# Row sums of masked spatial weights: a VectorE reduction with a round trip through DRAM in place of matmuls with ones

## The chip, the cores and the metric

The kernel runs on one core of one Trainium2 chip. The metric is the device time of one execution in microseconds (us). The engines are named as in the profile: PE (TensorE matmul), PEld (TensorE weight load), DVE (VectorE), ACT (ScalarE), POOL (GpSimd) and SP (SyncE, which issues most loads). Each engine works through its own instructions in program order and waits on semaphores of the others.

## The reference, cut to what matters

One decoder block for 512 positions of width 1024. Its combined input projection feeds two mixers. The change lies in mixer A, the spatial gating unit:

```
def chunked_gmlp(u, v, w_s, b_s, ln_g, ln_b):
    n = s // CHUNK                                   # 4 chunks of 128 positions
    v = layer_norm(v, ln_g, ln_b).reshape(bsz, n, CHUNK, A_GROUPS, A_GROUP_DIM)
    mask = jnp.tril(jnp.ones((CHUNK, CHUNK)))
    mixed = jnp.einsum('gts,bnsgc->bntgc', w_s * mask, v) + b_s.T[None, None, :, :, None]
    return u * mixed.reshape(bsz, s, A_WIDTH)
...
y_a = chunked_gmlp(gelu(a_u), gelu(a_v), gmlp_w_s, gmlp_b_s, gmlp_ln_g, gmlp_ln_b)
```

The layer norm's bias `ln_b` is the same for all positions. So its part of `mixed` is `ln_b[g, c]` times the sum over s of the masked `w_s[g, t, s]`. The kernel mixes only the normalized v, multiplies by `ln_g` afterwards, and adds a bias tile that holds `b_s[g, t] + ln_b[g, c] * rowsum[g, t]`. The change is about where the eight row-sum vectors of 128 come from and how they reach all 128 partitions.

## The kernel before, in words

All large products are done in three matmuls over split operands (`mm3`, lines 64 to 68): each fp32 operand is a rounded part `hi`, copied by ACT (line 134), and a remainder `lo`, subtracted by DVE or POOL (line 138). The weights come in chunks of 128x1024. `get` and `ensure` load up to three raw chunks ahead through SP and split a chunk two chunks before PE needs it, so what ACT, DVE, POOL and SP do is tied to the chunk that PE is at. The order on each engine is the order in which the program emits its instructions (`tc.manual_schedule()`); tables say at which chunk a small task is emitted.

The stretch of the change is this:

- The loop of lines 924 to 946 computes v (`a_v`) in two halves of 512 columns, four chunks each, with the token tile on the PSUM partitions: four banks 0 to 3 (tile name `pav`), one for each tile of 128 tokens. `VT` holds tasks for the eight chunks: loading the spatial weights (`load_ws`, `wmT`), masking them (`mask_ws`, on POOL), loading the bias rows (`load_bs`, `bsb`). After each half, ACT evacuates the four banks through a gelu (line 946).
- Then u (`a_u`) is computed in four groups of two chunks each by `opt_b` (calls in lines 1051 and 1052), with weights on the partitions. The groups use PSUM banks 0 and 1, then 2 and 3, and so on in turn (tile name `pb`). So the first group of u writes the banks from which the first two gelus of v read. For each chunk, `au_tasks` is emitted before the matmuls and `au_post` after them. Step 0 of `au_tasks` finishes the layer norm statistics (`ln_v`, then `rstd` on POOL), steps 1 and 2 apply it on ACT, step 3 finishes the bias tile (`bias_mix`). After the third chunk (step 2), `au_post` emits the two row-sum matmuls `rs_mm`. From step 3 on it emits the mixing matmuls (`mix_mm`), evacuated by DVE (`mix_ev`).
- In the background of the same chunks DVE runs a top-k (lines 766 and 770) and dot products for the modulation vectors (line 209). The operand of such a dot product, `mraw`, has one buffer in this stretch, so its next load is issued by SP when the last dot product is done.
- After u come seven products for the branch gates (`xround`, lines 1095 to 1138), which add and subtract intermediate sums in PSUM. One of them, `Z[1] + kept[3]` (line 1126), is done by DVE before the sixth product accumulates on it.

Of the kernel before, what the change touches and what calls it, by code (L numbers as in the profile page):

```python
# [9 lines left out]
F32 = mybir.dt.float32  # L10
# [16 lines left out]

@with_exitstack
def block_kernel(ctx: ExitStack, tc: tile.TileContext, x, x_t, c_row, positions, w_ada_t, w_first, w_in, w_blocks,
                 gmlp_w_s, gmlp_b_s, w_proj_a, w_proj_b,  # L30
                 w_out, w_ffn_in, w_ffn_out, final_norm_g, small, consts, out):
    nc = tc.nc
    T, V, A, P, SY = nc.tensor, nc.vector, nc.scalar, nc.gpsimd, nc.sync
# [262 lines left out]
    KZ = ([0, 1, 2, 3, 4, 5, 6, 7, 12, 13, 20], [8, 9, 10, 11, 16, 17, 18, 19, 14, 15, 21])  # L296
    NZ = 6

    wsum = {n: dram.tile([11 * 128, 512], F32, name=f"wsum{n}") for n in (1, 2, 3, 4)}
    gdr = {n: dram.tile([8, 128], F32, name=f"gdr{n}") for n in (2, 5)}  # L300
    W_Z = {}
# [306 lines left out]
    def rows_a(b):  # L608
        m = 32 * len(RB[b])
        rope_a(("r", b), rqt[b][:m], "q", m)  # L610

    def rows_b(b):
        rope_b(("r", b))
        for r, v in enumerate(RB[b]):
            P.dma_start(v, rqt[b][32 * r:32 * r + 32])
# [50 lines left out]
    def h_hi(key):  # L666
        HS[key] = h_home(key)
        A.activation(HS[key][0][0][0], h_part(key), AF.Copy)
# [230 lines left out]
    def mask_ws():  # L899
        P.affine_select(late["wmT"], late["wmT"], pattern=[[0, 8], [1, 128]], compare_op=OP.is_ge, fill=0.0, base=0,  # L900
                        channel_multiplier=-1)
        late["ones"] = mid.tile([128, 2, 128], F32, name="ones2", tag="ql", bufs=2)[:, 0]
        P.memset(late["ones"], 1.0)

    VT = {0: [load_ws, lambda: rows_a(1), lambda: rows_b(1)],
          1: [lambda: h_hi("S1"), lambda: h_hi("S4"), lambda: h_lo("S1"), lambda: h_lo("S4")],
          2: [lambda: rows_a(2), lambda: rows_b(2), lambda: h_hi("S3")],
          3: [lambda: h_lo("S3")],
          5: [mask_ws],
          7: [load_bs]}  # L910
    for _ in range(16):
        bg.append((1.4, topk_max))
# [11 lines left out]
    for h in range(2):  # L924
        pb = [bank(k, "pav") for k in range(4)]
        for i in W_AV[h]:
            for fn in VT.get(vs, []):
                fn()
            if vs % 2:
                x_move()  # L930
            if iu[1] < 24:
                idx_accs()
            else:
                run_bg(2.0)
            if vs in (5, 6):
                for tk in (2 * vs - 10, 2 * vs - 9):
                    ln_v(tk, 0)
            vs += 1
            hi, lo = get(i)
            for tk in range(4):  # L940
                opt_a_mm(pb[tk], tk, hi, lo, stream[i]["kts"], hT, 8)
            idx_mms(4 if vs > 2 else 3)
        if not vg:
            vg.extend(mid.tile([128, 2, D], F32, name=f"vg{i}", tag=f"P{i}", bufs=1) for i in range(2))
        for tk in range(4):
            A.activation(vg[tk // 2][:, tk % 2, h * 512:(h + 1) * 512], pb[tk], AF.Gelu_apprx_tanh)
# [33 lines left out]
            ylow.append(lambda: V.tensor_sub(yT[m][1], y, f(yT[m][0])))  # L980
        ylate.append((austep[0] - 1, hi))

    def rs_mm():
        late["rs"] = [bank(5 + k, "rs") for k in range(2)]
        for k, p in enumerate(late["rs"]):
            T.matmul(p, late["ones"], late["wmT"][:, 4 * k:4 * k + 4].rearrange("p a n -> p (a n)"), start=True, stop=True)

    def bias_mix():
        for m in range(8):
            b = late["bsb"][:, m]  # L990
            V.scalar_tensor_tensor(b, late["rs"][m // 4][:, 128 * (m % 4):128 * (m % 4) + 128], lnbc[:, m:m + 1], b,
                                   op0=OP.mult, op1=OP.add)

    ub = {}
    austep = [0, 0]
# [2 lines left out]
    def au_post():  # L998
        s = austep[1]
        austep[1] += 1  # L1000
        if s == 2:
            rs_mm()
        for m in AT.get(s, []):
            mix_mm(m)
        while ylate and ylate[0][0] < s:
            ylate.pop(0)[1]()

    def au_tasks():
        s = austep[0]
        austep[0] += 1  # L1010
        if s == 0:
            assert iu[1] == 24
            for tk in range(4):
                ln_v(tk, 1)
            rstd(rva, mva[:, :, 1], 4, 1.0)
            V.scalar_tensor_tensor(nmr, mva[:, :, 0], -1.0, rva, op0=OP.mult, op1=OP.mult)
        elif s < 3:
            ln_v2(2 * s - 2)
            ln_v2(2 * s - 1)
        elif s == 3:  # L1020
            bias_mix()
        while ylow:
            ylow.pop(0)()
        for m in AT.get(s - 1, []):
            mix_ev(m)
        while zlate:
            zlate.pop(0)()
        for _ in range(BG.get(s, 0)):
            run_bg(0.1)
        if s < 9:  # L1030
            x_move()
        elif s == 9:
            assert not xm
        elif s == 27:
            k_b()
        if s in (28, 29):
            at_split(s - 28)
# [961 lines left out]
    for tk in range(2):  # L1999
# [26 lines left out]
                finish(tk)  # L2026


_INS = ["x", "x_t", "c_row", "positions", "w_ada_t", "w_first", "w_in", "w_blocks", "gmlp_w_s", "gmlp_b_s",
        "w_proj_a", "w_proj_b", "w_out", "w_ffn_in", "w_ffn_out", "final_norm_g", "small", "consts"]  # L2030
_OUTS = [((1, 512, 1024), "float32")]

# [52 lines left out]
```

## Time and profile before

| what | value |
|---|---|
| time before, median of 3 runs | 797.27 us (793.59, 798.15, 797.27) |
| the profiled execution's own time | 795.42 us |
| span of the profiled execution | 793.5 us, mean granted TensorE clock 0.996 |
| busy: PE, PEld | 780.2 us (98%), 697.5 us (88%) |
| busy: DVE, ACT, POOL | 662.6 us (84%), 443.2 us (56%), 183.7 us (23%) |
| DMA | 155.05 MB, mean 195 GB/s |

The span is the time from the first to the last instruction that the profile holds; the execution's own time is 1.92 us longer. A share of busy time is a mean over the whole span. A row of the timeline has the start in us from the span's start, the duration, engine, line, operation, the written and read tiles, shapes, and how many instructions are merged; what stands in brackets at its end is the idle time of the engine before it and what ended it. Matmuls are pipelined: a 128x512 matmul is shown with 0.39 us, while the next one starts 0.23 us after it.

### The profile page before, as it was taken

The numbers are of one execution on the slowest core, as the hardware profiler recorded it, in microseconds if no ns is written. First come the engines' busy times: TensorE is split into PE (matmuls) and PEld (weight loads), VectorE is DVE, ScalarE is ACT, GpSimd is POOL, SyncE is SP. The second block draws the span as 40 slices with busy tenths as digits, with TensorE's granted clock in tenths as the row PEclk, the third lists the DMA queues.
The fourth block names the chain that finished last, engine by engine and source line by source line (L and its number), as shares of the span: only waits on it lengthen the run. The fifth ranks groups of instructions, "written<-read, shape, count | busy, mean of one in ns | idle before, by whom it ended". The sixth has DMA issues, their size and how long they took to land.

```text
span 793.5 us, 12600 instructions
## 1 busy us (share of the span) xinstructions
PE 780.2 (98%) x4747; PEld 697.5 (88%) x4747; DVE 662.6 (84%) x1114; ACT 443.2 (56%) x777; POOL 183.7 (23%) x220
## 2 busy tenths in 40 slices
PE   7999999999999999999999999999999999999996
PEld 6779988878998988988888899999999999878885
DVE  5988887678896899886788869899998888798877
ACT  6556445443453536666436576656655556576654
POOL 2064234574433401000020000313132122100001
PEclk9999999999999999999999999999999999999999
DMA  9949454889763733149682503989996977665764
GB/s 358 416 155 241 119 149 118 223 228 239 212 212 107 239 107 107 54 147 281 227 225 62 175 1 108 262 252 273 282 264 194 280 179 189 176 201 196 217 195 146
DMA packets 89886, 155.05 MB, mean 195 GB/s; under 512 B 7009, under 2 KB 54769, under 8 KB 89634
## 3 DMA queue, kind: packets, MB, share of 16 engines
q1 hardware_dynamic: 72976, 116.05, 44.3%
q0 software_dynamic: 15952, 37.17, 20.8%
q10 hardware_dynamic: 898, 1.04, 0.4%
q8 instruction: 37, 0.61, 0.3%
q14 instruction: 23, 0.19, 0.1%
HBM read 150.16 MB, written 33.56 MB: 232 GB/s over the span
## 4 chain that ended last, share of the span: by engine, by line
PE 78%; DVE 11%; ACT 4%; DMA 3%; issue 2%; POOL 0%; POOLq 0%; ACTq 0%; DVEq 0%; SPq 0%
PE R L66 7%; PE R L67 7%; PE R L68 7%; PE pb L66 7%; PE pb L67 7%; PE pb L68 7%; PE pfo L67 2%; PE pfo L68 2%; PE pfo L66 2%; DMA raw<-in_w_ffn_out_dram 2%; PE pav L66 2%; PE pav L67 2%; PE pav L68 2%; PE zx L1116 2%; PE zx L1119 2%
## 5 line engine op out<-in xcount | busy, mean ns | idle before, releaser
L134 ACT ACTIVATE hi<-raw 128x1024 fp32r<-128x1024 f32 (+1 forms) x111 | 114.4, 1031 | 80.5 <-PE pb L67 32.5
L138 DVE TENSOR_TENSOR lo<-raw,hi 128x1024 fp32r<-128x1024 f32 (+2 forms) x77 | 90.2, 1173 | 27.9 <-ACT hi L134 27.7
L138 POOL TENSOR_TENSOR lo<-raw,hi 128x1024 fp32r<-128x1024 f32 x27 | 69.0, 2558 | 101.1 <-ACT hi L134 70.4
L67 PE MATMUL pfo<-lo,za 128*128 128x512 f32 (+1 forms) x144 | 55.5, 385 | 0.2 <-DVE lo L138 0.2
L66 PE MATMUL pfo<-hi,za 128*128 128x512 f32 (+1 forms) x144 | 55.4, 385 | 0.0
L68 PE MATMUL pfo<-hi,za 128*128 128x512 f32 (+1 forms) x144 | 55.2, 384 | 0.0
L209 DVE CUSTOM_DVE_ANT_0 mraw<-mraw,scb,cols 128x1024 f32<-128x1024 f32 x24 | 37.6, 1566 | 11.1 <-DMA mraw<-in_w_ada_t_dram 11.1
L66 PE MATMUL R<-tb,sx 128*128 128x256 f32 x160 | 45.0, 281 | 0.3 <-ACT R L1820 0.3
L351 POOL COPY sm<-sm 128x1 f32<-128x1 f32 x36 | 26.4, 733 | 79.7 <-ACT sm L350 79.7
L67 PE MATMUL R<-tb,sx 128*128 128x256 f32 x160 | 44.6, 279 | 0.0
L68 PE MATMUL R<-tb,sx 128*128 128x256 f32 x160 | 44.6, 279 | 0.0
L66 PE MATMUL R<-tb,hi 128*128 128x256 f32 x160 | 44.6, 278 | 0.0
L67 PE MATMUL R<-tb,hi 128*128 128x256 f32 x160 | 44.6, 278 | 0.0
L68 PE MATMUL R<-tb,lo 128*128 128x256 f32 x160 | 44.6, 278 | 0.0
L66 PE MATMUL pb<-h,hi 128*128 128x512 f32 (+1 forms) x112 | 42.7, 381 | 0.0
L68 PE MATMUL pb<-h,lo 128*128 128x512 f32 (+1 forms) x112 | 41.9, 374 | 0.0
L67 PE MATMUL pb<-h,hi 128*128 128x512 f32 (+1 forms) x112 | 41.9, 374 | 0.0
L331 POOL DMA_DIRECT2D wsum<-in_w_ffn_out_dram x24 | 21.2, 885 | 76.0 <-DMA wsum<-wsum 42.0
L66 PEld LDWEIGHTS pfo<-hi,za 128*128 128x128 f32 x144 | 27.1, 188 | 6.1 <-ACT ps L1925 0.6
L67 PEld LDWEIGHTS pfo<-lo,za 128*128 128x128 f32 x144 | 27.1, 188 | 6.1 <-DVE lo L138 0.9
L68 PEld LDWEIGHTS pfo<-hi,za 128*128 128x128 f32 x144 | 27.1, 188 | 5.3
L66 PEld LDWEIGHTS R<-tb,sx 128*128 128x128 f32 x160 | 30.3, 189 | 0.7 <-ACT R L1820 0.5
(398 smaller groups left out, 2695.5 us busy)
## 6 DMA issues: line engine op xcount, KB each, us to landing
raw<-in_w_ffn_in_dram SPq DMA_DIRECT2D x44, 512.0 KB, 6.2
raw<-in_w_in_dram SPq DMA_DIRECT2D x30, 512.0 KB, 3.8
wsum<-in_w_ffn_out_dram POOLq DMA_DIRECT2D x30, 512.0 KB, 8.3
mraw<-in_w_ada_t_dram SPq DMA_DIRECT2D x24, 512.0 KB, 6.0
raw<-wsum SPq DMA_DIRECT2D x20, 512.0 KB, 3.7
s<-in_w_ada_t_dram SPq DMA_DIRECT2D x16, 512.0 KB, 8.8
raw<-in_w_ffn_out_dram SPq DMA_DIRECT2D x16, 512.0 KB, 4.6
xsum<-in_w_blocks_dram POOLq DMA_DIRECT2D x12, 512.0 KB, 6.4
```

What stands on the lines that cost most here:

```text
L66: T.matmul(o, wh, rh, start=start, stop=False, **kw)
L67: T.matmul(o, wh, rlo, start=False, stop=False, **kw)
L68: T.matmul(o, wlo, rh, start=False, stop=stop, **kw)
L134: A.activation(hi[:, :m], e["raw"][:, :m], AF.Copy)
L138: e["lo"].tensor_sub(lo[:, :m], e["raw"][:, :m], f(hi[:, :m]))
L209: V.tensor_tensor_reduce(out=raw[:, o], in0=raw[:, o], in1=c, scale=1.0, scalar=col if o.start else bias, op0=OP.mult, op1=OP.add, accum_o ...
L331: P.dma_start(wsum[n][o], src, accum_op=OP.add)
L351: P.tensor_copy(t, t)
L1116: T.matmul(Z[z][:, m], hi[:, j, cc], hh, start=start and j + m == 0, stop=False, skip_group_check=True)
L1119: T.matmul(Z[z][:, m], lo[:, j, cc], hh, start=False, stop=j == 3, skip_group_check=True)
```

## The change

A second copy of the spatial weights with the output position t on the partitions (`gmlp_w_n`, arranged by the host) is loaded by POOL (`load_wn`, emitted at chunk 2 of v) into the tile tag A1, masked by POOL (`mask_wn`, chunk 4), and summed over s by one DVE reduction (`row_sums`, chunk 6) into eight columns of `sm`. After the last matmuls of v, `rs_out` turns these columns into eight rows with a PE transpose, copies them with ACT to SBUF and writes them to DRAM from ACT's queue. At step 1 of u, `rs_in` reads them back on POOL's queue, broadcast to all partitions, as a 128x1024 tile in A1. `bias_mix` moves from step 3 to step 2 and becomes two DVE operations of 128x1024, in place of eight of 128x128 that read the row sums from PSUM. The two matmuls with ones, the memset of the ones and their PSUM banks go.

```diff
@@ mask_ws
-        late["ones"] = mid.tile([128, 2, 128], F32, name="ones2", tag="ql", bufs=2)[:, 0]
-        P.memset(late["ones"], 1.0)
+    def load_wn():
+        late["wn"] = mid.tile([128, 8, 128], F32, name="wn", tag="A1", bufs=1)
+        P.dma_start(late["wn"], gmlp_w_n)
+    def mask_wn():
+        P.affine_select(late["wn"], late["wn"], pattern=[[0, 8], [-1, 128]], compare_op=OP.is_ge, fill=0.0, base=0,
+                        channel_multiplier=1)
+    def row_sums():
+        V.tensor_reduce(sm[:, 0:8], late["wn"], op=OP.add, axis=AX.X)
+    def rs_out():
+        p = bank(7, "rsT")
+        T.transpose(p[:8, :128], sm[:, 0:8], ident)
+        gr = tiny.tile([128, 128], F32, name="gr", tag="gr", bufs=1)
+        A.activation(gr[:8], p[:8, :128], AF.Copy)
+        A.dma_start(rsd, gr[:8])
+    def rs_in():
+        late["rs"] = mid.tile([128, 8, 128], F32, name="rs", tag="A1", bufs=1)
+        P.dma_start(late["rs"], bass.AP(tensor=rsd.tensor, offset=rsd.offset, ap=[[0, 128], [128, 8], [1, 128]]))
@@ the loop over v, after the matmuls of a half and ahead of its gelus
+        if h:
+            rs_out()
@@
-    def rs_mm():
-        late["rs"] = [bank(5 + k, "rs") for k in range(2)]
-        for k, p in enumerate(late["rs"]):
-            T.matmul(p, late["ones"], late["wmT"][:, 4 * k:4 * k + 4].rearrange("p a n -> p (a n)"), start=True, stop=True)
     def bias_mix():
-        for m in range(8):
-            b = late["bsb"][:, m]
-            V.scalar_tensor_tensor(b, late["rs"][m // 4][:, 128 * (m % 4):128 * (m % 4) + 128], lnbc[:, m:m + 1], b,
-                                   op0=OP.mult, op1=OP.add)
+        V.tensor_mul(late["rs"], late["rs"], lnbc[:, :, None].to_broadcast([128, 8, 128]))
+        V.tensor_add(late["bsb"], late["bsb"], late["rs"])
@@ au_post
-        if s == 2:
-            rs_mm()
@@ au_tasks
-        elif s == 3:
+        if s == 1:
+            rs_in()
+        elif s == 2:
             bias_mix()
```

On ACT, where v ends and u begins, the rows before are these (`vg` is the gelu of v, `hi` the split of a weight chunk, `rl` an evacuation of the index scores):

```order
L750 ACTIVATE rl<-idx 128x256 x2
L134 ACTIVATE hi<-raw 128x1024
L946 ACTIVATE vg_1305<-pav 128x512 x2
L946 ACTIVATE vg_1306<-pav 128x512 x2
L134 ACTIVATE hi<-raw 128x1024
```

And this is the same place now:

```order
L751 ACTIVATE rl<-idx 128x256 x2
L134 ACTIVATE hi<-raw 128x1024
L919 ACTIVATE gr<-rsT 8x128
L920 DMA rsd<-gr 8x128
L971 ACTIVATE vg_1308<-pav 128x512 x2
L971 ACTIVATE vg_1309<-pav 128x512 x2
L134 ACTIVATE hi<-raw 128x1024
```

The copy of the turned row sums and the issue of their DMA stand ahead of all four gelus.

On PE the same place now reads as follows; the transpose stands between the last matmul of v and the first of u:

```order
L67 MATMUL pav<-lo,h_157 128x512
L68 MATMUL pav<-hi,h_159 128x512
L917 MATMUL rsT<-ident,sm 8x128
L66 MATMUL pb<-h_156,hi 128x512
L67 MATMUL pb<-h_158,hi 128x512
```

What ACT's copy waits for is thus an instruction that PE issues after all of v's matmuls.

On DVE, in the second and third chunk of u, the rows before are these (`mraw` is the dot product's operand, `m` and `sco` belong to the top-k):

```order
L209 ISA mraw,GG_88<-mraw,scb,cols 128x1024
L209 ISA GG_88 128x1
L991 SCALAR_TENSOR_TENSOR bsb<-rs,cols,bsb 128x128 x8
L766 MAX m_1696<-sco_640 128x8
L766 MAX m_1698<-sco_639 128x8
```

And now, one dot product and one round of the top-k earlier:

```order
L209 ISA mraw,GG_88<-mraw,scb,cols 128x1024
L209 ISA GG_88 128x1
L1009 TENSOR_TENSOR rs<-rs,cols 128x1024
L1010 TENSOR_TENSOR bsb<-bsb,rs 128x1024
L767 MAX m_1653<-sco_641 128x8
L767 MAX m_1655<-sco_640 128x8
```

The eight operations on PSUM rows have become two on SBUF tiles, behind the dot product of step 2.

## Rows read from the trace of the kernel before

**Rows 1.** The page: span and busy time of PE.
```profile
span 793.5 us, 12600 instructions
PE 780.2 (98%) x4747; PEld 697.5 (88%) x4747; DVE 662.6 (84%) x1114; ACT 443.2 (56%) x777; POOL 183.7 (23%) x220
```

**Rows 2.** Timeline of PE around the two row-sum matmuls.
```profile
172.29 0.39 PE L68 MATMUL pb<-h,lo 128*128 128x512 f32 x1
172.52 1.88 PE L986 MATMUL rs<-wmT,ones 128*128 128x512 f32 x4
...
174.46 0.40 PE L67 MATMUL pb<-h,hi 128*128 128x512 f32 x1
```

**Rows 3.** Timeline where v ends and u begins.
```profile
152.31 0.60 ACT L946 ACTIVATE vg<-pav 128x512 f32<-128x512 f32 x1
...
155.97 0.39 PE L68 MATMUL pav<-hi,h 128*128 128x512 f32 x1
...
156.42 0.39 PE L67 MATMUL pb<-h,hi 128*128 128x512 f32 x1
```

**Rows 4.** Timeline around another transpose with copy and DMA, of a modulation vector.
```profile
233.71 0.39 PE L68 MATMUL pb<-y,lo 128*128 128x512 f32 x1
233.93 0.27 PE L460 MATMUL mod<-ident,GG 128*8 128x128 f32 x1
234.24 0.27 ACT L462 ACTIVATE gr<-mod 8x128 f32<-8x128 f32 x1 [4.02 <-PE mod L460]
...
234.95 1.06 ACT L134 ACTIVATE hi<-raw 128x1024 fp32r<-128x1024 f32 x1 [0.44 <-ACT gr L462]
```

**Rows 5.** Timeline between the two halves of v.
```profile
130.98 2.07 ACT L946 ACTIVATE vg<-pav 128x512 f32<-128x512 f32 x4
...
131.63 0.19 PEld L66 LDWEIGHTS pav<-hi,h 128*128 128x128 f32 x1 [0.36 <-ACT vg L946]
...
131.97 0.39 PE L67 MATMUL pav<-lo,h 128*128 128x512 f32 x1
```

**Rows 6.** Timeline of the layer norm statistics and what follows them.
```profile
157.03 0.69 DVE L919 BATCH_NORM_STATS2 bst<-vg 128x6 f32<-128x512 f32 x1 [0.42 <-ACT vg L946]
...
157.75 0.21 DVE L921 BATCH_NORM_AGGREGATE mva<-bst 128x2 f32<-128x12 f32 x1
...
159.53 4.49 DVE L209 CUSTOM_DVE_ANT_0 mraw<-mraw,scb,cols 128x1024 f32<-128x1024 f32 x1
...
160.09 2.83 POOL L138 TENSOR_TENSOR lo<-raw,hi 128x1024 fp32r<-128x1024 f32 x1
```

**Rows 7.** DVE's groups by line and shape, 120 to 230 us: count, busy, mean ns, idle before.
```profile
L209 DVE CUSTOM_DVE_ANT_0 mraw<-mraw,scb,cols 128x1024 f32<-128x1024 f32 x9 | 18.4, 2048 | 8.8 <-DMA mraw<-in_w_ada_t_dram 8.8
...
L138 DVE TENSOR_TENSOR lo<-raw,hi 128x1024 fp32r<-128x1024 f32 x5 | 6.1, 1217 | 0.7 <-ACT hi L134 0.7
...
L673 DVE TENSOR_TENSOR hs<-xT,hs 128x1024 fp32r<-128x1024 f32 x1 | 3.4, 3430 | 0.0
...
L991 DVE SCALAR_TENSOR_TENSOR bsb<-rs,cols,bsb 128x128 f32<-128x128 f32 x8 | 2.1, 335 | 0.0
```

**Rows 8.** Timeline of DVE and PE around the sum that DVE adds in PSUM.
```profile
219.46 1.23 DVE L138 TENSOR_TENSOR lo<-raw,hi 128x1024 fp32r<-128x1024 f32 x1 [0.67 <-ACT hi L134]
...
221.21 0.69 DVE L1126 TENSOR_TENSOR zx<-zx,zk 128x512 f32<-128x512 f32 x1
...
222.82 0.28 PE L1116 MATMUL zx<-hs,hi 128*128 128x256 f32 x1
```

**Rows 9.** Timeline of POOL and DVE at the chunks of v.
```profile
135.75 2.75 POOL L138 TENSOR_TENSOR lo<-raw,hi 128x1024 fp32r<-128x1024 f32 x1 [6.02 <-ACT hi L134]
138.45 1.42 POOL L900 TENSOR_SCALAR_AFFINE_SELECT wmT<-wmT 128x1024 f32<-128x1024 f32 x1
...
151.11 1.07 DVE L753 SCALAR_TENSOR_TENSOR sco<-rl,wi,sco 128x256 f32<-128x256 f32 x2 [2.74 <-ACT rl L750]
```

**Rows 10.** DMA issues: size and median us from issue to landing.
```profile
bsb<-in_gmlp_b_s_dram POOLq DMA_DIRECT2D x1, 512.0 KB, 4.5
```

More of the change, by code (lines that the diff above doesn't have):

```diff
@@ L29, in block_kernel @@
 def block_kernel(ctx: ExitStack, tc: tile.TileContext, x, x_t, c_row, positions, w_ada_t, w_first, w_in, w_blocks,
-                 gmlp_w_s, gmlp_b_s, w_proj_a, w_proj_b,
+                 gmlp_w_s, gmlp_w_n, gmlp_b_s, w_proj_a, w_proj_b,
                  w_out, w_ffn_in, w_ffn_out, final_norm_g, small, consts, out):
@@ L297, in block_kernel @@
     NZ = 6
+    rsd = dram.tile([8, 128], F32, name="rsd")
     wsum = {n: dram.tile([11 * 128, 512], F32, name=f"wsum{n}") for n in (1, 2, 3, 4)}
@@ L901, in mask_ws @@
                         channel_multiplier=-1)
-        late["ones"] = mid.tile([128, 2, 128], F32, name="ones2", tag="ql", bufs=2)[:, 0]
-        P.memset(late["ones"], 1.0)
+    def load_wn():
[15 more added lines that the diff above has]
+        P.dma_start(late["rs"], bass.AP(tensor=rsd.tensor, offset=rsd.offset, ap=[[0, 128], [128, 8], [1, 128]]))
     VT = {0: [load_ws, lambda: rows_a(1), lambda: rows_b(1)],
           1: [lambda: h_hi("S1"), lambda: h_hi("S4"), lambda: h_lo("S1"), lambda: h_lo("S4")],
-          2: [lambda: rows_a(2), lambda: rows_b(2), lambda: h_hi("S3")],
+          2: [lambda: rows_a(2), lambda: rows_b(2), lambda: h_hi("S3"), load_wn],
           3: [lambda: h_lo("S3")],
+          4: [mask_wn],
           5: [mask_ws],
+          6: [row_sums],
           7: [load_bs]}
@@ L2026, in block_kernel @@
                 finish(tk)
-_INS = ["x", "x_t", "c_row", "positions", "w_ada_t", "w_first", "w_in", "w_blocks", "gmlp_w_s", "gmlp_b_s",
+_INS = ["x", "x_t", "c_row", "positions", "w_ada_t", "w_first", "w_in", "w_blocks", "gmlp_w_s", "gmlp_w_n", "gmlp_b_s",
         "w_proj_a", "w_proj_b", "w_out", "w_ffn_in", "w_ffn_out", "final_norm_g", "small", "consts"]
@@ L2072 @@
     given["gmlp_w_s"] = _np.asarray(inputs["gmlp_w_s"])[0].transpose(2, 0, 1)
+    given["gmlp_w_n"] = _np.asarray(inputs["gmlp_w_s"])[0].transpose(1, 0, 2)
     for name in _INS:
```

## The prediction

> **What bounds the kernel now.** I read the page first: PE is busy for 780.2 of 793.5 us [rows 1]. Then I read PE's timeline over the stretch from v to the gate branch (150 to 230 us): its matmuls follow each other without a gap, a 128x512 every 0.23 us. So there every 0.1 us that is taken from or put on PE's own sequence moves the end, and work on other engines counts only where PE comes to wait for it. Last I read the timelines of ACT, DVE and POOL in that stretch, to see how far ahead of PE they are.
>
> **What is removed from PE.** The last matmul before the row sums starts at 172.29, and the second one after them at 174.46 [rows 2]. Two steps between ordinary matmuls would be 0.45 us (155.97 to 156.42 is two such steps, rows 3). So the two row-sum matmuls (four instructions in the trace) cost 2.17 - 0.45 = 1.72 us, all of it on the path. This is what the change gives back.
>
> **What is added where v ends.** In the kernel before, the first gelu of v starts at 152.31, as soon as the first token tile is complete, while PE still works on the other three until 155.97; so u's first matmuls find banks 0 and 1 empty [rows 3]. Now a copy stands ahead of the gelus on ACT, and the copy waits for a transpose that PE issues after all of v's matmuls. ACT works in order, so all four gelus wait, and u's first matmul needs bank 0 from the first of them.
>
> The trace has both halves of that chain. The transpose of a modulation vector starts 0.22 us after the matmul before it, its copy 0.53 us after that same matmul, and ACT's next work, behind the DMA issue, 1.24 us after it [rows 4]. Between the halves of v PE already waits once for a gelu of this kind: the gelu starts at 130.98, PE's weight load is released at 131.63, and the second matmul starts at 131.97, 0.99 us after the gelu [rows 5]. Put together: last matmul of v 155.97, first gelu 155.97 + 1.24 = 157.21, second matmul of u 157.21 + 0.99 = 158.20, against 156.42 before [rows 3]. That is 1.78 us. The bank of the second output tile costs nothing more, since the four gelus of rows 5 take 2.07 us together, one every half microsecond, and PE spends three matmuls on the first bank.
>
> So the two terms on PE's own sequence cancel: -1.72 + 1.78 = +0.06 us. The bounds of the second term: 0.1 us if the gelus could pass the copy (the transpose's own slot on PE), and some 2.8 us if the DMA issue on ACT holds the gelus 1 us longer than in rows 4.
>
> **What the late gelus do to DVE.** The statistics of the four token tiles follow the gelus. Before, the last pair starts at 157.03 and 157.75, and DVE's dot product behind them at 159.53 [rows 6]. Now the first gelu ends at 157.81. Each tile takes 0.69 us for the statistics, 0.21 us for the aggregate and 0.1 us of starts, so 1.0 us; the last aggregate starts at about 161.6, 3.9 us later than before. The rsqrt on POOL, the dot product on DVE and the layer norm on ACT all move by these 3.9 us. Two things could then be late for PE.
>
> First the splits on POOL: the one that follows the statistics runs from 160.09 to 162.92 [rows 6], now from about 164.0 to 166.8. PE needs it in u's third chunk, which starts 23 steps of 0.227 us ahead of 172.29 [rows 2], at 167.1, and now 1.7 us later. That leaves 2 us, and the next splits have more: the broadcast read of the row sums, queued ahead of the next one, costs POOL an issue.
>
> Second the sums in PSUM. PE's sixth gate product starts at 222.82 and accumulates on a bank to which DVE adds at 221.21 for 0.69 us: done 0.92 us before. The split on which DVE waited just before was released by ACT after 0.67 us of idle time [rows 8]. So DVE may come to this place some 1.6 us late without any harm, and each further microsecond stops PE. Does DVE make up 3.9 us in 60? In this stretch it sits idle for 8.8 us, all of it waiting for the operand of the next dot product, in front of five of nine [rows 7]. But that operand has one buffer, and SP issues its load when the last dot product is done; a late one makes its successor's load late. So this idle time is no reserve, except where DVE's own work between two of them is longer than the load. I take 3.9 - 1.6 = 2.3 us, less 0.1 us for PE's own shift: 2.2 us of PE waiting at the sixth gate product. Bounds: 0 if the loads land faster, since the bias no longer stands in the interval where one was slowest, and 4.5 by the third rival.
>
> **The rest is covered.** The bias took DVE eight operations, 2.1 us; it becomes two of 128x1024 with two SBUF inputs, like the split of 1.22 us: 2.4 us [rows 7], one chunk earlier, while its reader is two chunks away. The reduction is one pass over 128x1024, which no row shows; its nearest row is that same 1.22 us, and bounds of 0.7 and 3.4 us (a statistics operation of half the width in rows 6, a delayed operation in rows 7) change little, as DVE idles for 2.74 us just after it [rows 9]. The second mask is 1.42 us on POOL and lies in 6.02 us of idle time [rows 9]; if that cover went, the split of 2.75 us behind it would move by 1.4 us. The broadcast read comes after a write of 4 KB, issued at about 157; the like broadcast of the bias rows landed in 4.5 us [rows 10]. It is issued at about 167, so lands at 172, and DVE asks for it behind its dot product at about 175: no wait, unless it takes 8 us. The chip reads 1 MB more, as two loads of 512 KB, some 9 us of one transfer's time against 74 us of traffic between 123 and 197; raw chunks are loaded two chunks ahead. I count nothing for it.
>
> **A rule against this change.** In this trace a two-input DVE operation of 128x1024 took 3.43 us instead of 1.22 us [rows 7]; it was one that ran beside a POOL split. The eight old operations, with one input in PSUM, took 335 ns each. The Trainium skill ("SBUF — State Buffer", section "Who interferes with whom") says that a DVE instruction with two SBUF inputs and a GpSimd instruction that reads SBUF shut each other out for a whole instruction. By that rule the new form of the bias is exposed where the old was not, and the trace agrees in those 3.43 us; what it would cost is the third rival below.
>
> **The sum.** 793.5 - 1.72 + 1.78 + 2.2 = 795.8 us of span, +2.3 us. The profiled execution itself took 795.42 us, below the median of 797.27 and above the lowest of 793.59. The four times of this kernel have a mean of 796.1 us, and I add the 2.3 us to that: 798.4 us.
>
> **The rivals.**
> 1. DVE makes up its delay, since the load of the operand takes less time than the work between two dot products once the bias has left that interval. Then only +0.06 us stays: 796.2 us. For it speaks that the longest interval held both the bias and the wait. Against it: four other intervals also end in a wait for the load.
> 2. The gelus do not hold PE for 1.78 us, because the copy or the DMA issue on ACT lets them start earlier; the row sums' 1.72 us come through, and DVE is hardly late: 794.4 us. Against it speak the order on ACT and rows 4 and 5.
> 3. Slower: DVE meets POOL's splits in the new place. The bias pair at about 175 runs beside a split of the fifth or sixth chunk, and one of its two operations takes 3.43 instead of 1.22 us, so DVE is late by 3.9 + 0.3 + 2.2 = 6.4 us. PE then waits 6.4 - 1.6 - 0.1 = 4.7 us at the sixth gate product: 800.9 us. It decides once DVE is over 5.5 us late there. For it: POOL has a split in every chunk of u. Against it: a split fills only about half of a chunk's 5.4 us, and DVE must come second.
>
> **How the numbers follow.** My forecast (PE waits 1 to 3.5 us at the gate product) has a chance of 0.50, by itself 797.0 to 799.8 us; the first rival 0.24, the second 0.09, the third 0.17. A measurement of this kernel can tell about 0.5%, 4 us, from no change. Forecast and first rival lie within it, and nearly all of the second; of the third four fifths are beyond it. With the spread of the runs shown (793.59 to 798.15) on top I give faster 0.04, same 0.78, slower 0.18. The range reaches from the second rival's time to a little above the third's: 794.4 to 802.5 us.
>
> **What would show it.** In the changed kernel's profile: no row-sum matmuls; all four gelus of v's second half back to back after the copy, and a wait of u's first weight load for a gelu, with u's second matmul 2.2 us after v's last (0.45 before); the reduction without a wait of PE behind it; the dot product behind the statistics at about 163.4; and a wait of the sixth gate product for DVE's sum, the only one of more than 0.5 us. I am wrong if that first gap is under 1 or over 3 us, if PE waits for POOL's third-chunk split, if DVE waits for the row sums to land, or if PE passes the sixth gate product without a wait.

## The result, and the profile after

The changed kernel takes 798.7 us (median of 20 runs, 794.22 to 805.67), the kernel before 794.19 us (20 runs beside it, 791.39 to 798.15). The ratio is 1.0060 with a 95% interval of 1.0040 to 1.0081, that is 4.8 us (3.2 to 6.4) slower. The forecast was +2.3 us. It came to nearly the measured time because it was put on a mean of 796.1 us, which lies 1.9 us above the median of the larger sample: two errors of about 2 us that cancel. So the nearness of the time is luck: the change itself is about twice the +2.3 us that was forecast, and +2.3 us lies below its interval. The middle of the ratio lies beyond the 0.5% that I had called no change, and its interval reaches from below that mark to above it.

The profiled execution took 798.21 us (795.42 before). Its page:

```profile
span 796.4 us, 12592 instructions
...
PE 778.9 (98%) x4744; PEld 696.6 (87%) x4744; DVE 665.2 (84%) x1109; ACT 442.9 (56%) x778; POOL 184.3 (23%) x222
```

PE is busy 1.3 us less and the span is 2.9 us longer [rows 1]. Since one execution differs from the next by some us over its 800, I compare a stretch in which all that the change does lies: from v's last matmul (L68 in both kernels) to the last block of eight matmuls of the gate product that the prediction calls the sixth. Before it is 71.56 us, from 155.97 [rows 3] to the second of these rows of PE's timeline (the first is used below):

```profile
219.05 1.11 PE L1119 MATMUL zx<-h,lo 128*128 128x256 f32 x8
...
227.53 1.11 PE L1119 MATMUL zx<-h,lo 128*128 128x256 f32 x8
```

After it is 232.70 - 155.75 = 76.95 us, so 5.39 us longer. What follows the stretch lies outside the change and took between 561.1 us (e2) and 567.1 us (e12) in the fourteen profiled executions, 566.0 before and 563.7 after; that is why the two spans differ by 2.9 us only. PE's timeline after:

```profile
155.75 0.39 PE L68 MATMUL pav<-hi,h 128*128 128x512 f32 x1
155.98 0.27 PE L917 MATMUL rsT<-ident,sm 128*8 128x128 f32 x1
157.59 0.50 PE L66 MATMUL pb<-h,hi 128*128 128x512 f32 x1 [1.34 <-ACT vg L971]
157.93 0.40 PE L67 MATMUL pb<-h,hi 128*128 128x512 f32 x1
...
218.81 1.10 PE L1137 MATMUL zx<-h,lo 128*128 128x256 f32 x8
221.47 0.39 PE L1134 MATMUL zx<-hs,hi 128*128 128x256 f32 x1 [1.55 <-ACT zx L1121]
...
226.44 0.35 PE L1134 MATMUL zx<-hs,hi 128*128 128x256 f32 x1 [1.79 <-DVE zx L1144]
...
228.97 1.91 PE L1137 MATMUL zx<-hs,lo 128*128 128x256 f32 x8
...
232.70 1.07 PE L1137 MATMUL zx<-h,lo 128*128 128x256 f32 x8
```

The reader is to see three things. The hold at u is there: from v's last matmul to u's second 2.18 us, against 0.45 [rows 3], so +1.73 us, which the missing row-sum matmuls [rows 2] give back. At 218.81 PE begins a block 0.24 us earlier than before (219.05), and it had ended v 0.22 us earlier (155.75 against 155.97), so hold and row sums have cancelled. Then come two waits, one for ACT at the product ahead of the sixth and one for DVE's sum at the sixth. And behind them a block of eight matmuls takes 1.91 us instead of 1.10: the granted clock falls, which the stretches of the profile show (the columns are window, its length, busy time of PE, PEld, DVE, ACT and POOL with instructions, granted clock, DMA share, GB/s; the third window is the second half of the one above it):

```profile
222.00:226.00 4.00, 2.65 (x22) 2.42 (x21) 4.00 (x4) 3.97 (x5) 1.40 (x1) 1.00 0.33 111
226.00:230.00 4.00, 3.56 (x21) 3.59 (x22) 4.00 (x11) 2.42 (x4) 3.65 (x2) 0.71 0.80 287
228.00:230.00 2.00, 2.00 (x11) 2.00 (x11) 2.00 (x7) 0.60 (x1) 2.00 (x2) 0.50 0.87 335
230.00:234.00 4.00, 4.00 (x31) 3.96 (x30) 4.00 (x7) 1.74 (x3) 1.47 (x1) 0.86 0.74 224
```

Before, the second of these windows has a clock of 1.00 and no idle time of PE:

```profile
226.00:230.00 4.00, 4.00 (x30) 3.74 (x29) 4.00 (x5) 2.72 (x4) 1.65 (x1) 1.00 0.68 207
```

Worked out from where the products begin, before against after: 1.84 us at the first wait, 2.02 us at the second, and 1.55 us for the time at the lower level of the clock (0.50 is 1.2 GHz, 1.00 is 2.4 GHz). Together 5.4 us. ACT's and DVE's timelines after tell where the waits come from:

```profile
156.29 0.27 ACT L919 ACTIVATE gr<-rsT 8x128 f32<-8x128 f32 x1 [4.21 <-PE rsT L917]
156.59 0.31 ACTq L920 DMA_DIRECT2D rsd<-gr  x1
156.94 2.07 ACT L971 ACTIVATE vg<-pav 128x512 f32<-128x512 f32 x4 [0.38 <-ACT gr L919]
...
218.86 0.60 ACT L1125 ACTIVATE zk<-zx 128x512 f32<-128x512 f32 x1 [3.72 <-DVE y L1005]
...
220.83 0.58 ACT L1121 ACTIVATE zx<-zx 128x512 f32<-128x512 f32 x1
```

```profile
162.43 4.51 DVE L209 CUSTOM_DVE_ANT_0 mraw<-mraw,scb,cols 128x1024 f32<-128x1024 f32 x1
...
174.76 1.40 DVE L209 CUSTOM_DVE_ANT_0 mraw<-mraw,scb,cols 128x1024 f32<-128x1024 f32 x1 [4.84 <-DMA mraw<-in_w_ada_t_dram]
...
176.10 1.21 DVE L1009 TENSOR_TENSOR rs<-rs,cols 128x1024 f32<-128x1024 f32 x1
177.40 1.23 DVE L1010 TENSOR_TENSOR bsb<-bsb,rs 128x1024 f32<-128x1024 f32 x1
...
188.78 1.29 DVE L209 CUSTOM_DVE_ANT_0 mraw<-mraw,scb,cols 128x1024 f32<-128x1024 f32 x1 [2.46 <-DMA mraw<-in_w_ada_t_dram]
...
225.60 0.69 DVE L1144 TENSOR_TENSOR zx<-zx,zk 128x512 f32<-128x512 f32 x1
```

The four gelus run back to back behind the copy. The dot product behind the statistics starts at 162.43, 2.9 us later than before [rows 6]; the load of the next operand lands 7.8 us after that dot product ends (6.0 before: 164.0 to 170.0); and DVE's sum comes at 225.60, 4.4 us later than before [rows 8]. ACT's copy that seeds the product ahead of the sixth is late too: the copy of zk in front of it waits 3.72 us for a buffer that DVE's late subtraction of y frees (`zk` and `y` share a ring of buffers).

### The profile page after: what moved, and what is told of

Same layout as the page of the kernel before. It is cut to its first block, busy times and chain, and to the rows that moved or that the text cites. A ratio compares the mean times of both kernels' runs of the same rounds, so it can differ in the third digit from the quotient of the medians.

```text
span 796.4 us, 12592 instructions
## 1 busy us (share of the span) xinstructions
PE 778.9 (98%) x4744; PEld 696.6 (87%) x4744; DVE 665.2 (84%) x1109; ACT 442.9 (56%) x778; POOL 184.3 (23%) x222
## 4 chain that ended last, share of the span: by engine, by line
PE 58%; DVE 10%; DMA 4%; ACT 3%; issue 2%; POOL 0%; SPq 0%; POOLq 0%; DVEq 0%
PE R L66 8%; PE R L67 8%; PE R L68 8%; PE pfo L66 4%; PE pfo L67 4%; PE pfo L68 4%; PE pb L67 4%; PE pb L68 4%; PE pb L66 4%; DMA mraw<-in_w_ada_t_dram 3%; PE pgb L66 2%; PE pgb L68 2%; PE pgb L67 1%; PE zx L1137 1%; PE zx L1134 1%
## 5 line engine op out<-in xcount | busy, mean ns | idle before, releaser
L68 PE MATMUL pfo<-hi,za 128*128 128x512 f32 (+1 forms) x144 | 55.2, 383 | 0.0
L352 POOL COPY sm<-sm 128x1 f32<-128x1 f32 x36 | 23.9, 664 | 89.2 <-ACT sm L351 89.2
L68 PE MATMUL R<-tb,sx 128*128 128x256 f32 x160 | 44.4, 278 | 0.0
L68 PE MATMUL R<-tb,lo 128*128 128x256 f32 x160 | 44.4, 277 | 0.0
L68 PE MATMUL pb<-h,lo 128*128 128x512 f32 (+1 forms) x112 | 41.9, 374 | 0.0
L68 PEld LDWEIGHTS pfo<-hi,za 128*128 128x128 f32 x144 | 27.1, 188 | 5.4
```

The source lines that it names most:

```text
L68: T.matmul(o, wlo, rh, start=False, stop=stop, **kw)
L352: P.tensor_copy(t, t)
```

## The experiments

Twelve kernels were run (e1 to e13; there is no e3). My theory was that the order on ACT makes the whole loss, by way of DVE. Rival A was the added traffic, rival B the new place of the bias. "Stretch" and "zx waits" (PE's waits at those two products) are from each kernel's one profiled execution; ratios are to the kernel before, from 6 to 20 runs each, and carry the verdicts.

| kernel | stretch us | zx waits us | ratio, 95% |
|---|---|---|---|
| before | 71.56 | none | 1 |
| changed | 76.95 | 1.55 + 1.79 | 1.0060 (1.0040 to 1.0081) |
| e1 gelus first | 73.59 | 1.26 + 1.78 | 1.0027 (1.0009 to 1.0045) |
| e2 before, copy ahead of gelus | 78.57 | 1.44 + 1.78 | 1.0097 (1.0078 to 1.0117) |
| e4 before, two loads | 76.64 | 1.79 + 0.35 | 1.0025 (1.0003 to 1.0047) |
| e5 changed, bias a step later | 81.04 | 2.00 + 1.79 | 1.0113 (1.0095 to 1.0132) |
| e6 gelus first, no traffic | 74.32 | 1.79 + 0.35 | 1.0024 (1.0002 to 1.0047) |
| e7 changed, no traffic | 76.16 | 1.99 + 0.69 | 1.0049 (1.0022 to 1.0077) |
| e8 e1, read a step earlier | 74.39 | 0.64 + 1.79 | 1.0012 (0.9989 to 1.0035) |
| e9 e1, sums a step later | 73.40 | 1.24 + 1.78 | 1.0045 (1.0019 to 1.0071) |
| e10 both of these | 70.73 | 0.71 | 0.9998 (0.9981 to 1.0016) |
| e11 e10, copy inside v | 74.88 | 1.99 + 1.81 | 1.0039 (1.0015 to 1.0062) |
| e12 e11, read still earlier | 73.70 | 1.52 + 1.78 | 1.0052 (1.0030 to 1.0074) |
| e13 e10, copy ahead of gelus | 75.33 | 1.57 + 1.80 | 1.0041 (1.0022 to 1.0060) |

The profiled execution of e2 (797.54 us) was the fastest of its runs, those of e4 (799.76) and e8 (798.81) the slowest or nearly so, so their stretches stand beside their ratios with care. PE has further waits ahead of mixing matmuls or earlier products in e4 (0.88 us), e5 (3.1 us in sum), e7 (0.35 us) and e11 (0.64 us).

**e1: the gelus ahead of the copy.**

```
+        (the four gelus of this half)
         if h:
             rs_out()
```

> The changed kernel with the transpose and copy of the row sums moved behind the four gelus of v's second half; all else (both loads of 512 KB, the reduction, the new bias) stays. Measure: the stretch on PE from the last matmul of v to the fourth block of the zx sums of the sixth gate product (155.97 to 227.53 in the kernel before, 71.56 us; 155.75 to 232.70 after the change, 76.95 us), the waits of PE for zx, and the ratio to the kernel before. Theory (the order on ACT is the cause): u's second matmul again about 0.5 us after v's last (plus 0.1 to 0.3 us for the transpose), LN dot product near 159.5, no wait of PE for zx over 0.3 us, granted clock 1.00 throughout 150 to 240, stretch about 70 us, so 1.5 us less than before and 0.2% faster than it. Rival A (the added 1 MB of traffic slows the operand's loads): the hold at u goes but waits for zx of 1 us or more stay; stretch about 74 to 75 us. Rival B (the new form or place of the bias makes DVE late): as rival A, with the lateness of DVE beginning behind the two bias operations rather than at the loads.

The hold went: u's second matmul follows v's last after 0.57 us (2.18 in the changed kernel). The stretch fell by 3.4 us, but not below that of before: both waits stayed, and the kernel is 0.27% slower than before. So by the middles of the ratios the order on ACT costs 2.6 us, though the two intervals just overlap, and something else another 3.7 us against my forecast for this run (2.1 us slower instead of 1.6 us faster).

**e2 and e4: one suspect alone, in the kernel before.** e2 adds only the transpose, copy and write ahead of the gelus:

```
+        if h:
+            T.transpose(p[:8, :128], cols[:, 0:8], ident)
+            A.activation(gr[:8], p[:8, :128], AF.Copy)
+            A.dma_start(held, gr[:8])
```

> The kernel before, with its row-sum matmuls and its old bias, and with a transpose of eight columns, a copy on ACT and a write of 4 KB put ahead of the four gelus of v's second half (what is written is read by nothing). Neither load of 512 KB is added. Theory (order on ACT): u's second matmul 2.2 us after v's last, the LN dot product about 3 us later than before, PE waits of 1.5 us or more in sum for zx at the fifth and sixth gate product, with or without a fall of the granted clock behind them; stretch 71.56 + 1.7 + 3.5 to 5.5 = about 77 to 79 us, time 0.6 to 0.9% above before. Rivals A and B (traffic; bias): only the hold of 1.7 us; no wait for zx over 0.5 us; stretch about 73.3 us, time 0.2% above before.

e4 adds only the two loads, `P.dma_start(wn, gmlp_w_s)` in v's third chunk and the broadcast read of 512 KB in u's second step:

> The kernel before with the two additional loads of 512 KB alone, issued where the change issues them (a copy of the spatial weights in v's third chunk; a broadcast read of 4 KB to 128 partitions in u's second step), into a buffer that nothing reads. Theory (order on ACT): no hold, DVE on time, no wait of PE for zx over 0.5 us, stretch 71.5 us +- 0.3, time within 0.2% of before. Rival A (traffic): the operand's load in that stretch takes some 8 instead of 6 us, DVE comes 2 us or more late to the sums, PE waits for zx for 1 to 3 us or more, stretch 73 to 76 us, time 0.2 to 0.6% above before.

PE's waits in e2, then in e4 (total us, times, longest):

```profile
PE zx L1123 <- DVE zx L1133: 1.8, 1, 1.8
PE zx L1123 <- ACT zx L1110: 1.4, 1, 1.4
PE pb L66 <- ACT vg L953: 1.3, 1, 1.3
```

```profile
PE zx L1126 <- ACT zx L1113: 1.8, 1, 1.8
PE mix L973 <- DVE y L981: 0.9, 1, 0.9
```

Each is enough by itself to bring the wait at the product ahead of the sixth. e2 came out as the theory said, at 1.0097 a little above it: the late gelus alone, with no added load, cost no less than the whole change, even with the 1.72 us taken off that the row-sum matmuls still cost in e2. In e4 the gelus were on time and the load behind the first dot product landed after 7.4 us instead of 6.0, as rival A said; its stretch of 76.64 is from an execution of 799.76 us, and by the runs the loads cost 0.25% (0.03 to 0.47%). So in the kernel before, either way of making DVE late soon reaches PE.

**e5: the bias where it stood before** (`if s == 3` in place of `s == 2`).

> The changed kernel with the two bias operations put back into u's fourth step, where the eight old ones stood. Theory (order on ACT): the hold of 1.7 us and the late LN chain stay, and with them PE waits for zx of 1.5 us or more in sum; stretch about 75 to 78 us; time within 0.3% of the changed kernel. Rival B (place of the bias): without the bias in the earlier interval DVE gets back to its old times, the waits for zx go, the stretch is about 71.6 + 0 to 0.5 us, and the time that of the kernel before.

Rival B fell, and the other way round: with the bias in its old step the kernel is 1.13% slower. The earlier place gives some 4 us back (1.0113 against 1.0060, intervals apart). That is more than my theory's 0.3%: with the bias late, PE also waits 0.57 and 1.62 us ahead of mixing matmuls, for the operation on DVE that reads the bias tile, and 0.95 us ahead of an earlier gate product. That is the part of the first rival of the prediction which was true.

**e6 and e7: the traffic taken out of the changed kernel.** The mask reads the first copy of the weights, and the broadcast brings one block, with the gelus first (e6) and with the copy first (e7).

```
-        P.dma_start(late["wn"], gmlp_w_n)
+        (mask_wn reads late["wmT"] instead)
-        P.dma_start(late["rs"], ...[[0, 128], [128, 8], [1, 128]])
+        P.dma_start(late["rs"][:, 7:8], ...[[0, 128], [128, 1], [1, 128]])
```

> The gelus ahead of the copy, as in the first experiment, and without the added traffic: the second copy of the weights is taken by the mask from the first one (no load, so the sums are of the wrong triangle), and the broadcast read brings one block of 64 KB, which the first bias operation reads for all eight blocks; every operation on DVE, ACT and POOL keeps its shape. What differs from the reference is the row sums. Theory as the first four runs leave it (the late gelus and the added broadcast each make DVE late by themselves): with both gone the loads of the operand take 6.0 us, the dot product behind the statistics starts near 159.5 and takes 4.5 us, no wait of PE for zx over 0.5 us, clock 1.00, stretch from v's last matmul to the gate product 70.0 +- 0.5 us, time 0.2% below before. Rival C (it is the transpose, the reduction or the new bias, not traffic, that stays in the first experiment): waits for zx of 2 to 3 us and a stretch of 72 to 73.5 us, as there.

> The changed kernel, its copy ahead of the gelus, without the added traffic, in the same way (the row sums differ from the reference). Theory: the hold of 1.7 us at u stays and the dot product behind the statistics is 2.9 us late, but the load behind it takes 6.0 instead of 7.8 us; DVE is some 3 instead of 4.5 us late at the last sum, and the waits for zx come to 1 to 2.5 us instead of 3.3, with no or a shorter fall of the granted clock; stretch 73 to 75 us (76.95 in the changed kernel, 71.56 before), time 0.1 to 0.4% above before. Rival D (the late gelus alone make the whole loss, the traffic adds nothing to it): stretch 76.5 to 77.5 us and 0.6%.

Rival A is not borne out for the changed kernel. Without the traffic the operand's load behind the first dot product still took 8.0 us (e6) and 8.2 us (e7) from that dot product's end, and the ratios are those of e1 and of the changed kernel within their intervals, so that the traffic's share, if any, is not resolved. Both theories of mine missed: e6 is 0.24% above before and not 0.2% below, and e7's stretch of 76.16 us lies nearer to rival D's than to mine. In e6 the wait went from DVE's sum to ACT's seed copy and the clock fell behind it; rival C was right that a stretch above 72 us stays. So the bytes of the added loads are not what makes that load long. The loads into xsum that POOL issues were slower in that stretch too (a median of 7.7 us between 160 and 176 us in e7, against 6.0 before). What sets these times stays open.

**e8 to e10: where the reduction and the broadcast stand.** e1's trace gave the lead. Its rows of DVE, then of POOL:

```profile
144.64 1.21 DVE L913 TENSOR_REDUCE sm<-wn 128x8 f32<-128x1024 f32 x1
...
160.25 7.46 DVE L209 CUSTOM_DVE_ANT_0 mraw<-mraw,scb,cols 128x1024 f32<-128x1024 f32 x1 [0.85 <-DMA mraw<-in_w_ada_t_dram]
```

```profile
147.81 2.46 POOL L138 TENSOR_TENSOR lo<-raw,hi 128x1024 fp32r<-128x1024 f32 x1 [6.52 <-ACT hi L134]
...
160.18 2.82 POOL L138 TENSOR_TENSOR lo<-raw,hi 128x1024 fp32r<-128x1024 f32 x1
```

e8 is e1 with the read issued at u's first step (`if s == 0: rs_in()`), e9 is e1 with the reduction at v's last chunk (`7: [row_sums, load_bs]`), e10 has both.

> The full computation: gelus ahead of the copy, and the broadcast read of the row sums issued one step earlier, ahead of the split of u's third chunk, so that it flies while DVE is in the dot product behind the statistics and no operand is being loaded. Theory: the loads of the operand behind it take about 6 us, the dot product starts ahead of the split and takes 4.5 us (7.46 in the first experiment), waits for zx under 0.5 us in sum, stretch 70 to 71 us, time 0.1 to 0.2% below before. Rival C: as in the first experiment, waits of 2 to 3 us, stretch 72 to 73.5 us, 0.2 to 0.3% above before.

> The full computation, as the first experiment (gelus ahead of the copy), and DVE's reduction one step later, where DVE waits for ACT for 1.7 us. Theory E, from the traces so far: the reduction at 144.6 delays DVE's next operations by 0.84 us, with them ACT's copy, POOL's split (147.81 instead of 146.97) and the raw load that waits for the split's buffer (150.7 instead of 149.8); this load stands ahead of the operand's load, which lands 0.9 us later, so that the dot product behind the statistics starts at 160.25, just behind POOL's split at 160.18, and takes 7.46 instead of 4.49 us. With the reduction moved, the split is back at 146.8, the dot product starts at 159.4 without a wait for its load and takes 4.5 us, DVE's last sum before the sixth gate product comes 3 us earlier, waits for zx 0 to 1 us (2.6 to 3.1 in the first experiment), stretch 70 to 71.5 us, time 0.1 to 0.2% below before. Rival F (the operand's loads are late for other reasons, any new order of the transfers will do): the dot product starts in time, the loads behind it still take 7 to 8 us, waits for zx of 1.5 to 3 us stay, stretch 72 to 74 us, time 0.1 to 0.3% above before.

> As the run before it, with the broadcast read issued one step earlier as well. Theory E: the dot product behind the statistics in time and short, no load of the operand in flight together with the broadcast, stretch 70 to 71 us, waits for zx under 0.5 us, time 0.1 to 0.3% below before, the best of all. Rival F: stretch 72 to 74 us, time of before or 0.2% above.

e8 came out at 1.0012, which cannot be told from the kernel before, nor from e10 below; neither its theory's gain nor rival C's loss is shown. In its profile the dot product behind the statistics took 1.29 us, but the next one met a split and took 5.17 us.

The head of theory E was right. In e9 the split is back at 146.67 and the dot product starts on time. But the gain was lost right behind it, as rival F said. e9's DVE rows:

```profile
159.31 4.53 DVE L209 CUSTOM_DVE_ANT_0 mraw<-mraw,scb,cols 128x1024 f32<-128x1024 f32 x1
...
171.41 3.18 DVE L209 CUSTOM_DVE_ANT_0 mraw<-mraw,scb,cols 128x1024 f32<-128x1024 f32 x1 [4.60 <-DMA mraw<-in_w_ada_t_dram]
...
175.82 3.25 DVE L1009 TENSOR_TENSOR bsb<-bsb,rs 128x1024 f32<-128x1024 f32 x1
```

The load took 7.6 us, and then the dot product and the bias addition each met a split on POOL (171.12 and 175.22) and took 3.2 us instead of 1.3. The time of e9, 0.45% above before, is no better than e1's. In e10 POOL waits 1.5 us for the row sums' write, so its split starts at 162.26, DVE's dot product goes through ahead of it, and the load behind starts 3 us earlier:

```profile
159.57 1.28 DVE L209 CUSTOM_DVE_ANT_0 mraw<-mraw,scb,cols 128x1024 f32<-128x1024 f32 x1
...
164.33 4.89 DVE L209 CUSTOM_DVE_ANT_0 mraw<-mraw,scb,cols 128x1024 f32<-128x1024 f32 x1 [0.51 <-DMA mraw<-in_w_ada_t_dram]
...
221.30 0.69 DVE L1143 TENSOR_TENSOR zx<-zx,zk 128x512 f32<-128x512 f32 x1
```

Here the stretch is 0.83 us shorter than before, roughly the 1.72 us of the row sums less 0.12 us for the transpose and 0.71 us of waiting. By its runs e10 beats the changed kernel (0.9998 against 1.0060, intervals apart) and cannot be told from the kernel before, so the forecast gain of 0.1 to 0.3% is not shown.

**e11 to e13: variants of e10.** e11 puts transpose and copy ahead of v's last chunk (with the transpose in PSUM bank 4 instead of 7), e12 also issues the read ahead of the rsqrt, and e13 puts the copy back ahead of the gelus.

```
e11  +  if vs == 7:
     +      rs_out()
e12  +  rs_in()        (ahead of ln_v of u's first step)
e13     rs_out() ahead of the gelus, as in the changed kernel
```

> The full computation: reduction one step later, transpose, copy and write of the row sums inside v's last chunk (ahead of its matmuls, so that nothing stands between v's last matmul and the gelus), broadcast read one step earlier. Theory: no hold at u at all and the write has landed when the broadcast is issued, so that POOL no longer waits 1.5 us for it; the splits behind it are 1.5 us earlier than in the run before. Stretch 70.0 to 71 us, waits for zx under 0.7 us, time 0.1 to 0.3% below before. Against it: the split starting earlier meets DVE's dot product again, which then takes 4.5 instead of 1.28 us, so that the next load starts 3 us later, with the broadcast still in flight; then waits for zx of 1.5 to 3 us, stretch 72 to 74 us, time 0.1 to 0.4% above before.

> As the run beside it, with the broadcast read issued ahead of the rsqrt on POOL, some 3 us earlier. Theory: the broadcast is done before the load of the next operand starts; but it now flies beside the load of the operand for the dot product behind the statistics. If that load still lands before 159.4: stretch 70 to 71 us, time 0.1 to 0.3% below before. If it lands later than POOL's split begins: the dot product takes 7 us as in the first experiment, waits for zx of 2 to 3 us, stretch 72 to 74 us, 0.2 to 0.4% above before.

> The full computation: the changed kernel with the copy ahead of the gelus as it stood, and only the reduction one step later and the broadcast read one step earlier (the placement with which the gelus-first version took the time of the kernel before). It tells what the order on ACT costs by itself in that placement, and what the placement gives the changed kernel. Theory (the order costs its hold of 1.6 us on PE and, by the late layer norm, another 1 to 2.5 us at the gate products): u's second matmul 2.2 us after v's last, the write lands before POOL asks for it (POOL comes 3 us later), stretch 73.5 to 75 us (70.73 with the gelus first, 76.95 in the changed kernel), time 0.3 to 0.5% above before. Rival G (placement is all; DVE makes up the late layer norm): stretch 72.0 to 72.8 us, that is only the hold on top, time 0.1 to 0.2% above before. Rival H (placement gives nothing while the gelus are late): stretch 76.5 to 77.5 us, 0.6%.

e11 and e12 went the way of what stood against them. In e11 POOL no longer waits, its split starts at 161.13, and the dot product takes 7.41 us again; in e12 it is the small operation ahead of the dot product that meets the split and takes 3.50 us instead of 0.16. That alone does not make e12 late, though: three dot products on, at 184.95, DVE is 0.5 us behind the kernel before. The delay that stays comes from the dot product at 190.59, which runs beside a POOL split (190.36) and takes 3.23 us, and from the load behind it:

```profile
184.95 1.28 DVE L209 CUSTOM_DVE_ANT_0 mraw<-mraw,scb,cols 128x1024 f32<-128x1024 f32 x1 [3.23 <-DMA mraw<-in_w_ada_t_dram]
...
190.59 3.23 DVE L209 CUSTOM_DVE_ANT_0 mraw<-mraw,scb,cols 128x1024 f32<-128x1024 f32 x1
...
200.46 1.29 DVE L209 CUSTOM_DVE_ANT_0 mraw<-mraw,scb,cols 128x1024 f32<-128x1024 f32 x1 [2.32 <-DMA mraw<-in_w_ada_t_dram]
```

In the kernel before, these three start at 184.46, 190.13 and 197.34. e13 against e10 gives the order on ACT by itself: 0.43% or 3.4 us, the intervals just apart, with a hold at u of 2.17 us. The time is what the theory said, and the stretch is 4.6 us longer, of which 1.6 us is the hold. DVE's rows in e13:

```profile
162.41 1.28 DVE L209 CUSTOM_DVE_ANT_0 mraw<-mraw,scb,cols 128x1024 f32<-128x1024 f32 x1
...
170.77 1.28 DVE L209 CUSTOM_DVE_ANT_0 mraw<-mraw,scb,cols 128x1024 f32<-128x1024 f32 x1 [4.10 <-DMA mraw<-in_w_ada_t_dram]
...
173.29 3.25 DVE L1009 TENSOR_TENSOR bsb<-bsb,rs 128x1024 f32<-128x1024 f32 x1
...
188.63 1.29 DVE L209 CUSTOM_DVE_ANT_0 mraw<-mraw,scb,cols 128x1024 f32<-128x1024 f32 x1 [4.66 <-DMA mraw<-in_w_ada_t_dram]
...
225.61 0.69 DVE L1143 TENSOR_TENSOR zx<-zx,zk 128x512 f32<-128x512 f32 x1
```

DVE's sum came at 225.61, as in the changed kernel; so rival G fell, and for DVE rival H was right: with the gelus late the better placement gives it nothing. But the way there is another one. The dot product behind the statistics ends at 163.7, no later than before (164.0), and the next starts 4.0 us earlier than in the changed kernel. The delay comes back behind it, with the bias addition beside a split and a load of 7.6 us that lands just ahead of 188.63 (5.4 us, just ahead of 188.78, in the changed kernel). So no single long load explains why DVE's sum is 4.4 us late with the gelus late. The stretch is 1.6 us shorter than the changed kernel's, about what the time at the lower clock had cost there; in this execution the clock did not fall.

## Why the prediction came out as it did

- **The row sums on PE and the hold at u** (-1.72 and +1.78 us): right. The hold was +1.73 us, and PE's lead on the kernel before was 0.22 us at the end of v and 0.24 us at 218.81, so the two terms cancelled to 0.02 us. e1 and e13 show that the copy ahead of the gelus makes it.
- **The late layer norm** (3.9 us): its size was wrong, 2.9 us. The four statistics, once nothing held them, followed at 0.80 us and not at 1.0. POOL's split behind them was in time for PE, as predicted.
- **PE's wait at the sixth gate product** (2.2 us, bounds 0 to 4.5): this is the step that was mis-sized. Its mechanism was there, and it cost 5.4 us in the profiled execution: the two waits 3.9 us, within its bounds, and with the clock beyond them. Three things are in place of the one term. DVE did not carry its 2.9 us unchanged to the sum but came 4.4 us late. I had taken the times of the loads as given, and they were not: the first behind the late dot product took 7.8 instead of 6.0 us, the next 5.9 instead of 3.7, the third 5.4 instead of 6.4. Why the sum comes out at 4.4 us stays open, since e13 ends there by another way. PE had to wait one product earlier too, for ACT's seed copy, which waited for a buffer of DVE: I had followed DVE's sum alone and not the buffers that DVE frees. And the granted clock fell behind the two waits.
- **The signs**: the first gap (2.18 us) and the wait of the sixth gate product came as stated, but that wait was not the only one of more than 0.5 us, and the dot product behind the statistics started at 162.4 and not at 163.4.
- **The rest is covered**: the reduction took 1.21 us, the bias pair 2.44 us, and PE waited for neither. But DVE's idle time behind the reduction was no free cover: e1 and e9 show that in the seventh chunk the reduction delays a POOL split by 0.84 us and with it the next load.
- **"I count nothing" for the traffic**: no cost of it is resolved in the changed kernel (e1 against e6, the changed kernel against e7), though in e4 loads of the same size make DVE late in the kernel before.
- **The rivals.** The first (DVE makes up its delay) fell. The second (the gelus not held) fell by the same rows as the hold. The third (the bias meets POOL's split) did not occur in the changed kernel, whose two operations took 1.21 and 1.23 us; its loss of 4.8 us is the measured one, but that came by another way. Its mechanism is real: in e9 the addition took 3.25 us beside a split. The Trainium skill ("SBUF — State Buffer", section "Who interferes with whom") says that a DVE instruction with two SBUF inputs contends with a GpSimd instruction that reads SBUF, and that the order of issue decides which of them blocks. The rows agree on the contention, the dot product taking 1.28 us with no split beside it (e10), 4.5 us beside one (e9) and 7.4 us beside two (e11). They do not show the order: in e9 the dot product starts at 159.31, ahead of the split at 159.91, and takes 4.53 us all the same.

## What to carry to other kernels

A small copy put ahead of larger work on an in-order engine costs what all that work's readers lose, so put it behind that work, even where the copy's own result is wanted soon. Where an engine off the critical path waits for a load that it triggers itself through a single buffer, do not count its idle time as a reserve, and give the delay that it carries on wide bounds to both sides: in these runs it grew (2.9 to 4.4 us in the changed kernel), and it came back after it had been made up (e13). Follow the buffers that the engine frees as well as the values it makes. In such a schedule each small step moves which of two engines comes first at a shared place, so an edit is to be judged by runs of several placements, not of one.

## What was not expected of the hardware

- The granted clock fell to the lower level behind the waits at the gate products in the profiled executions of the changed kernel, e2, e4, e5, e6, e7 and e8, and not in those of e1, e9, e11, e12 and e13, whose waits are as long (1.26 + 1.78, 1.99 + 1.81 and 1.57 + 1.80 us in e1, e11 and e13). The sizes of these waits do not tell the two apart, and what does stays open. It cost 1.55 us in the changed kernel.
- The load of 512 KB issued at the end of the dot product behind the statistics landed between 3.4 us (e8, 161.6 to 165.0) and 8.2 us (e7) after its buffer came free. It is not a matter of bytes alone: between 160 and 176 us e7 moved 167 GB/s on the mean, with fewer loads issued, and the kernel before 236.
- DVE's dot product of 128x1024 is shown to begin 0.47 us (e11) and 0.60 us (the changed kernel) ahead of a POOL split, and still takes 7.41 us (two splits) and 4.51 us (one) instead of 1.28. Where it begins 2.7 us ahead (e10) it takes 1.28 us.
